# Moving the matmul operands of a decoder trunk to multiples of 256 bytes

## The chip, the cores and the metric

The kernel runs on one core of one Trainium2 chip. The metric is the device time of one execution in microseconds (us), the median over runs. The profile is one further execution, recorded by the hardware profiler.

## The reference

One decoder layer on x of 1024 positions by 1024 channels, float32. Cut to what matters:

```python
h = layer_norm(x, ln_in_g, ln_in_b)
u = h @ w_in                       # GLU halves a, g | z | x,B,C | dt | gate_a | gate_b
y_a = conformer_branch(u_glu, ...) # a*sigmoid(g), causal 31-tap depthwise conv, LN, silu, @ w_conv_out
y_b = ssd_branch(z, xbc, dt, ...)  # 4-tap conv, silu, Mamba-2 state space scan, gated RMS norm, @ w_ssm_out
mix = (sigmoid(gate_a) * y_a + sigmoid(gate_b) * y_b) @ w_o
h = layer_norm(ALPHA * h + mix, ln1_g, ln1_b)
up = causal_dwconv(h @ w_up, dw_w, dw_b)          # 1024 -> 2 * 2816 channels, 3 taps
ffn = (silu(up_gate) * up_val) @ w_down           # 2816 -> 1024
out = layer_norm(ALPHA * h + ffn, ln2_g, ln2_b)
```

## The kernel before

**Numbers as pairs.** Every large operand is kept as two halves of type `float32r`, a rounded high part and the rest (`weights` at L150, `split_to` at L181, `split_pair` at L738). A product is three matmuls (`mm3` at L164, lines 167 to 169): high by high, high by low, low by high. In `TE.matmul(ps, wa, xa)` the first operand is stationary (128 columns, loaded into the array by a LDWEIGHTS that the profile lists as PEld) and the second is moving: 512 columns streamed past it, except in `first_columns` (L349), where it is 256.

**Stages.** The positions go in two halves. For each half: `ln_in` normalises and transposes into `hT`; `mixers` runs the projections of `hT`, the 4-tap convolutions, the state space groups (`ssd_group`) and, on VectorE, the 31-tap convolution (`conv31`, L421); `combine` makes `sT` and multiplies `sT` by `w_co` and `yT` by `w_sp`. Then `out_proj` (first half) and `ffn_blocks` (second half), which also prepares the feed-forward input in blocks: `h1b1` and `h1b2` (tiles of pool `big`) and three block sums `h1s1` to `h1s3`. `up_first` and 22 calls of `up_pair` make the up projection in seven block products (a Strassen-like scheme with 4 chunks of contraction, so 12 matmuls each); their PE order is written out by hand (`tc.manual_schedule`). One of the seven uses the weights `w_s3`, which lie in pool `up`. `down` runs seven more products over 11 contraction steps each; a step takes one weight tile for both operands and 12 matmuls, and the tiles come in turn from `wsp` (left) and from pool `down` (right). `ln_out` ends the kernel.

**Order.** The framework's scheduler orders the instructions of each engine, with the priorities given in the code. Loads of weights go through SP's DMA queue.

**Where the tiles lie.** SBUF space of each partition is given out by a stack of pools from the left (the first pool begins at byte 16512) and another stack from the right (down from byte 229344). Each tile's size is rounded up to 32 bytes. A pool that is closed gives its space to the next; a tile that comes to lie on an older one waits for that one's last use. With the sizes of the code the tiles begin here, in bytes modulo 256:

| tiles | pool, side | before |
|---|---|---|
| `ident` | const, left | 128 |
| `pc` (2276 bytes, slot of 2304) | const, left | 160 |
| `hT`, `yT`, `mixT`, `h1b1`, `h1b2` | big, left | 160 |
| staged weights `st`, `ra`, `rb`, `dr` | wst, left | 160 |
| weights `w_*` | wsp, left | 160 |
| `sT` | comb, left | 160 |
| weights `w_s3` | up, left | 32 |
| block sums `h1s1` to `h1s3` | ffq, right | 224 |
| weights of every second step of `down` | down, right | 224 |
| `seg_mv`, `seg_st`, `state0` to `state3` | states, right | 224 |

All offsets within these tiles that a matmul of 512 columns uses are multiples of 512 bytes.

Lines that the prediction's steps touch: `pc` L125 and its load L251, the loads of `x` L244 and `nw` L204, the store of `x` L258, the weight loads L153, the first reader of `pc` L265.

Of the kernel before, what the change touches and what calls it, by code (L numbers as in the profile page):

```python
# [8 lines left out]
F32 = mybir.dt.float32  # L9
# [7 lines left out]
P = 128  # L17
# [24 lines left out]
PC_N = PC_FB + 44  # L42
# [14 lines left out]
def kernel(  # L57
# [15 lines left out]
    V, A, G, TE, SY = nc.vector, nc.scalar, nc.gpsimd, nc.tensor, nc.sync  # L73

    def pool(name, bufs=1, **kw):
        return tc.tile_pool(name=name, bufs=bufs, reuse_waits="tile", **kw)

    const = ctx.enter_context(tc.tile_pool(name="const", bufs=1))
# [13 lines left out]

    ident = const.tile([P, P], F32, name="ident")
    make_identity(nc, ident)
    mean_stack = ExitStack()
    mean_w = mean_stack.enter_context(pool("mean", side="right")).tile([P, P], F32, name="mean_w")
    V.memset(mean_w, 1.0 / D)
# [24 lines left out]
    V.tensor_add(kind_st, kind[:, 0:1], kind[:, 1:2])  # L122
    kind_neg = const.tile([P, 2], F32, name="kind_neg")
    V.tensor_scalar_mul(kind_neg, kind[:, 0:2], -1.0)
    pc = const.tile([P, PC_N], F32, name="pc")  # L125
    a_log = statep.tile([P, HEADS], F32, name="a_log")
    dskip = statep.tile([P, HEADS], F32, name="dskip")
    u_halo = statep.tile([P, 24, 3], F32, name="u_halo")
# [32 lines left out]
    def big_tile(name):  # L161
        return big.tile([P, 2, KD, HALF], F32R, tag="big", name=name)
# [25 lines left out]
    def transpose_to(dst, src, t, k0, n):  # L188

        for q in range(0, n, 4):  # L190
            pt = bank(0)
            for i in range(4):
                TE.transpose(
                    pt[:, i * P : (i + 1) * P], src[:, (q + i) * P : (q + i + 1) * P], ident
                )
            pv = pt.rearrange("p (k t) -> p k t", k=4)
            hi = dst[:, 0, k0 + q : k0 + q + 4, t * P : (t + 1) * P]
            lo = dst[:, 1, k0 + q : k0 + q + 4, t * P : (t + 1) * P]
            A.copy(hi, pv)
            V.tensor_tensor(out=lo, in0=pv, in1=hi.bitcast(F32), op=ALU.subtract)  # L200

    def row(pl, start, n, name, tag=None):
        r = pl.tile([P, n], F32, tag=tag or name, name=name)
        SY.dma_start(r, prow[start : start + n].partition_broadcast(P))  # L204
        return r
# [4 lines left out]
    def ln_stats(pl, tiles, name, sts=None):  # L210

        n = len(tiles)
        mv = pl.tile([P, n, 2], F32, tag="ln_mv", bufs=2, name=f"mv_{name}")
        rs = pl.tile([P, n], F32, tag="ln_rs", bufs=2, name=f"rs_{name}")
        for i, t in enumerate(tiles):
            if sts:
                st = sts[i]
            else:
                st = pl.tile([P, 2, 6], F32, tag="ln_st", bufs=2, name=f"st_{name}{i}")
                for q in range(2):  # L220
                    ln_part(pl, t, st, q)
            V.bn_aggr(out=mv[:, i, :], in_=st)  # L222
        A.activation(out=rs, in_=mv[:, :, 1], func=AF.Sqrt, bias=eps)
        V.reciprocal(out=rs, in_=rs)
        return mv, rs

    def ln_apply(t, mv, rs, i, g, b):
        V.scalar_tensor_tensor(  # L228
            out=t, in0=t, scalar=mv[:, i, 0:1], in1=g, op0=ALU.subtract, op1=ALU.mult
        )  # L230
        V.scalar_tensor_tensor(  # L231
            out=t, in0=t, scalar=rs[:, i : i + 1], in1=b, op0=ALU.mult, op1=ALU.add
        )

    def ln_in(hh):
        hT = big_tile(f"hT{hh}")
        with pool(f"lnin{hh}", side="right") as pl:
            first = hh == 0
            xts, gb = [], []
            with tc.high_priority(offset=6000):  # L240
                for t in range(4):
                    xt = pl.tile([P, D], F32, tag="x", bufs=4, name=f"x{hh}_{t}")
                    r0 = hh * HALF + t * P
                    SY.dma_start(xt, x[r0 : r0 + P, :])  # L244
                    xts.append(xt)
                    if first and t == 1:
                        gb = [row(pl, RW_ING, D, "in_g"), row(pl, RW_INB, D, "in_b")]
            if not first:
                gb = [row(pl, RW_ING, D, "in_g"), row(pl, RW_INB, D, "in_b")]
            if first:  # L250
                SY.dma_start(pc, pcol)  # L251
                SY.dma_start(a_log, prow[RW_AL : RW_AL + HEADS].partition_broadcast(P))
                SY.dma_start(dskip, prow[RW_SD : RW_SD + HEADS].partition_broadcast(P))
            for t, xt in enumerate(xts):
                with tc.high_priority(offset=(6000 - 1000 * (t // 2)) if first else 0):
                    mv, rs = ln_stats(pl, [xt], f"in{hh}_{t}")
                    ln_apply(xt, mv, rs, 0, *gb)
                    SY.dma_start(h_scr[hh][t * P : (t + 1) * P, :], xt)  # L258
                    transpose_to(hT, xt, t, 0, KD)
        return hT  # L260
# [861 lines left out]
    def ln_out(dp, t, r, g, b, st):  # L1122

        with tc.high_priority(offset=200 if t == 7 else 0):
            mv, rstd = ln_stats(dp, [r], f"f{t}", [st])
            halves = [slice(q * HALF, (q + 1) * HALF) for q in range(2)]
            for cs in halves:
                ln_apply(r[:, cs], mv, rstd, 0, g[:, cs], b[:, cs])
                SY.dma_start(out[t * P : (t + 1) * P, cs], r[:, cs])

    hT = ln_in(0)
    yT = mixers(0, hT)
    mixT = combine(0, hT, yT)
    hT = ln_in(1)
    with pool("rows0") as pl:
        rs = [pl.tile([P, D], F32, name=f"r0_{t}") for t in range(4)]
# [134 lines left out]
```

## Time and profile before

| | us |
|---|---|
| median of 3 runs (2006.31, 2008.04, 2008.36) | 2008.04 |
| the profiled execution | 2007.04 |
| its span, first to last instruction | 2005.2 |
| TensorE matmuls busy (PE, 9164) | 1971.1 |
| TensorE weight loads busy (PEld, 9164) | 1620.4 |
| VectorE busy (DVE) | 1693.9 |
| ScalarE busy (ACT) | 1022.5 |
| GpSimd busy (POOL) | 178.0 |

PEld overlaps PE. Matmuls are pipelined: the duration of one runs over into the next, so the step from one start to the next is the shorter number that fills the span. The ends of matmuls are modelled, the starts are recorded. POOL's spans are rough. The granted clock is the share of full speed that the throttle gave TensorE; its mean here is 0.998.

### The profile page before, as it was taken

How to read it: one execution, taken by the hardware profiler on the slowest of the kernel's cores; microseconds unless marked ns; L12 is line 12 of the kernel's file. 1: busy time of each engine (PE TensorE's matmuls, PEld its weight loads, DVE VectorE, ACT ScalarE, POOL GpSimd, SP SyncE). 2: the span in 40 equal slices, each digit the busy share in tenths (PEclk: the TensorE clock that was granted, in tenths of full speed). 3: DMA queues.
4: the chain of work that ended last, by engine and by line, in shares of the span. 5: the costliest groups of instructions: out<-in, count | busy, mean ns of one | idle time of the engine just before them, and what ended most of it. 6: DMA issues, size and time to landing. Idle time of an engine off the chain costs nothing. (4 is left out here: it accounts for less than half of the span.)

```text
span 2005.2 us, 24594 instructions
## 1 busy us (share of the span) xinstructions
PE 1971.1 (98%) x9164; PEld 1620.4 (81%) x9164; DVE 1693.9 (84%) x2261; ACT 1022.5 (51%) x1480; POOL 178.0 (9%) x144
## 2 busy tenths in 40 slices
PE   7999999999999999999999999999999999999998
PEld 6888888888888888888888888877778888888886
DVE  7599999979865868999998977578998878778768
ACT  4465654556453265665545546255554444553432
POOL 2010101001300000100000122001000000011000
PEclk9999999999999999999999999999999999999999
DMA  6223223233445532222323253487442232368573
GB/s 222 88 70 95 79 87 123 85 111 106 168 128 183 221 109 74 84 90 85 115 90 111 100 173 121 131 283 250 146 158 104 100 121 95 106 217 266 184 241 110
DMA packets 97031, 272.20 MB, mean 136 GB/s; under 512 B 11216, under 2 KB 11216, under 8 KB 96912
## 3 DMA queue, kind: packets, MB, share of 16 engines
q1 hardware_dynamic: 88992, 246.78, 37.2%
q0 software_dynamic: 5616, 19.66, 2.7%
q10 hardware_dynamic: 2304, 4.20, 0.6%
q8 instruction: 72, 1.18, 0.3%
q14 instruction: 47, 0.39, 0.1%
HBM read 221.05 MB, written 49.55 MB: 135 GB/s over the span
## 5 line engine op out<-in xcount | busy, mean ns | idle before, releaser
L421 DVE SCALAR_TENSOR_TENSOR c<-v,pc,c 128x512 f32<-128x512 f32 x480 | 374.5, 803 | 6.4 <-ACT c L410 5.0
L479 POOL TENSOR_TENSOR au<-seg_mv,head_of 128x1024 fp32r<-128x1024 f32 x32 | 77.0, 2408 | 958.5 <-PE sm L488 728.2
L167 PE MATMUL acc<-hT,w_c 128*128 128x512 f32 x352 | 141.1, 401 | 0.0
L168 PE MATMUL acc<-hT,w_c 128*128 128x512 f32 x352 | 140.7, 400 | 0.0
L169 PE MATMUL acc<-hT,w_c 128*128 128x512 f32 x352 | 138.5, 393 | 0.0
L910 DVE SCALAR_TENSOR_TENSOR fo<-u,pc,fo 128x1024 f32<-128x1024 f32 x88 | 111.4, 1285 | 0.4 <-ACT fo L906 0.4
L376 DVE SCALAR_TENSOR_TENSOR xbc<-u,pc,xbc 128x512 f32<-128x512 f32 x144 | 109.6, 773 | 0.7 <-ACT xbc L374 0.5
L167 PE MATMUL acc<-h1s,w_s 128*128 128x512 f32 x264 | 104.5, 396 | 2.3 <-ACT u L894 2.3
L169 PE MATMUL acc<-h1s,w_s 128*128 128x512 f32 x264 | 104.0, 394 | 0.0
L168 PE MATMUL acc<-h1s,w_s 128*128 128x512 f32 x264 | 103.5, 392 | 0.0
L167 PE MATMUL acc<-w_z,hT 128*128 128x512 f32 x256 | 100.9, 401 | 0.0
L168 PE MATMUL acc<-w_z,hT 128*128 128x512 f32 x256 | 100.9, 394 | 0.0
L169 PE MATMUL acc<-w_z,hT 128*128 128x512 f32 x256 | 100.7, 396 | 0.0
L155 ACT CAST w_c<-st_c 128x1024 fp32r<-128x1024 f32 x50 | 52.6, 1052 | 88.9 <-PE acc L169 68.1
L1049 ACT CAST w_dn<-dr 128x1024 fp32r<-128x1024 f32 (+1 forms) x73 | 60.8, 842 | 71.9 <-DVE dr L979 31.1
L1050 DVE TENSOR_TENSOR w_dn<-dr,w_dn 128x1024 fp32r<-128x1024 f32 (+1 forms) x73 | 70.1, 967 | 14.8 <-ACT w_dn L1049 14.6
L168 PEld LDWEIGHTS acc<-hT,w_c 128*128 128x128 f32 x352 | 66.1, 188 | 17.0 <-issue 3.8
L169 PEld LDWEIGHTS acc<-hT,w_c 128*128 128x128 f32 x352 | 66.1, 188 | 16.2 <-issue 2.6
L167 PEld LDWEIGHTS acc<-hT,w_c 128*128 128x128 f32 x352 | 66.1, 188 | 16.0 <-issue 2.6
L156 DVE TENSOR_TENSOR w_c<-st_c,w_c 128x1024 fp32r<-128x1024 f32 x47 | 60.5, 1288 | 20.2 <-ACT w_c L155 20.2
L167 PE MATMUL sm<-h1b,w_s 128*128 128x512 f32 x176 | 69.6, 396 | 0.0
L169 PE MATMUL sm<-h1b,w_s 128*128 128x512 f32 x176 | 69.3, 394 | 0.0
(354 smaller groups left out, 5703.1 us busy)
## 6 DMA issues: line engine op xcount, KB each, us to landing
st_c<-wcol SPq DMA_DIRECT2D x50, 512.0 KB, 3.5
st_z<-wz SPq DMA_DIRECT2D x32, 512.0 KB, 3.5
st_wo<-wo SPq DMA_DIRECT2D x24, 512.0 KB, 4.0
ra<-wup SPq DMA_DIRECT2D x22, 512.0 KB, 3.5
rb<-wup SPq DMA_DIRECT2D x22, 512.0 KB, 3.4
t_scr<-fo POOLq DMA_DIRECT2D x22, 512.0 KB, 3.4
dr<-t_scr SPq DMA_DIRECT2D x44, 256.0 KB, 4.0
dr<-wdown SPq DMA_DIRECT2D x38, 256.0 KB, 4.3
```

The costliest lines, as they stand in the source:

```text
L155: A.copy(w[:, 0, :], st)
L156: (eng or V).tensor_tensor(out=w[:, 1, :], in0=st, in1=w[:, 0, :].bitcast(F32), op=ALU.subtract)
L167: TE.matmul(ps, wa(0), xa(0), start=start, stop=False, skip_group_check=more)
L168: TE.matmul(ps, wa(0), xa(1), start=False, stop=False, skip_group_check=more)
L169: TE.matmul(ps, wa(1), xa(0), start=False, stop=stop, skip_group_check=more)
L376: V.scalar_tensor_tensor(out=o, in0=u[:, k : k + HALF], scalar=pc[:, wc + k : wc + k + 1], in1=o, op0=ALU.mult, op1=ALU.add,)
L421: V.scalar_tensor_tensor(out=accs[i], in0=v[:, k : k + HALF], scalar=pc[:, wc + k : wc + k + 1], in1=accs[i], op0=ALU.mult, op1=ALU.add,)
L479: G.tensor_tensor(out=au, in0=seg_mv[:, c, :].unsqueeze(1).to_broadcast([P, 8, P]), in1=head_of[:, g, :].unsqueeze(2).to_broadcast([P, 8, P]),
L910: V.scalar_tensor_tensor(out=o, in0=u[:, k : k + T], scalar=pc[:, wc + k : wc + k + 1], in1=o, op0=ALU.mult, op1=ALU.add,)
L1049: A.copy(w[:, 0, cs], src)
L1050: V.tensor_tensor(out=w[:, 1, cs], in0=src, in1=w[:, 0, cs].bitcast(F32), op=ALU.subtract)
```

## The change

Two pools grow by unused bytes. `pc`, the last tile of the left pool `const`, gets 24 more columns (2372 bytes, a slot of 2400 instead of 2304), and its load fills the first 569 columns as before. A new pool `edge` of 56 columns (224 bytes), which nothing reads or writes, is the first on the right side. Every tile left of the middle that is allocated after `pc` moves up by 96 bytes, every tile on the right down by 224. `ident` and the other tiles ahead of `pc` stay.

| tiles, bytes modulo 256 | before | after |
|---|---|---|
| `hT`, `yT`, `mixT`, `h1b1`, `h1b2`, `sT`, staged and split weights | 160 | 0 |
| block sums, weights of `down` on the right, states, `seg_mv`, `seg_st` | 224 | 0 |
| weights `w_s3` | 32 | 128 |

```diff
@@ -92,6 +92,8 @@
 
     ident = const.tile([P, P], F32, name="ident")
     make_identity(nc, ident)
+    edge = ctx.enter_context(pool("edge", side="right"))
+    edge.tile([P, 56], F32, name="edge")
     mean_stack = ExitStack()
     mean_w = mean_stack.enter_context(pool("mean", side="right")).tile([P, P], F32, name="mean_w")
     V.memset(mean_w, 1.0 / D)
@@ -122,7 +124,7 @@
     V.tensor_add(kind_st, kind[:, 0:1], kind[:, 1:2])
     kind_neg = const.tile([P, 2], F32, name="kind_neg")
     V.tensor_scalar_mul(kind_neg, kind[:, 0:2], -1.0)
-    pc = const.tile([P, PC_N], F32, name="pc")
+    pc = const.tile([P, PC_N + 24], F32, name="pc")
     a_log = statep.tile([P, HEADS], F32, name="a_log")
@@ -248,7 +250,7 @@
             if first:
-                SY.dma_start(pc, pcol)
+                SY.dma_start(pc[:, :PC_N], pcol)
                 SY.dma_start(a_log, prow[RW_AL : RW_AL + HEADS].partition_broadcast(P))
```

## The prediction

> **What bounds the kernel now.** I read the page first, then the waits of TensorE, then busy time by stage, then the matmuls of single tiles with their start times.
>
> ```profile
> span 2005.2 us, 24594 instructions
> PE 1971.1 (98%) x9164; PEld 1620.4 (81%) x9164; DVE 1693.9 (84%) x2261; ACT 1022.5 (51%) x1480; POOL 178.0 (9%) x144
> PEclk9999999999999999999999999999999999999999
> ```
>
> ```profile
> PE sm L193 <- DVE x L231: 14.8, 3, 12.2
> PE acc L167 <- ACT u L894: 2.3, 2, 1.2
> ```
>
> ```profile
> 100.00:510.00 410.00, 410.00 (x1965) 336.06 (x1964) 398.56 (x542) 237.84 (x374) 35.80 (x15) 1.00 0.30 96
> 700.00:1100.00 400.00, 399.82 (x1910) 328.90 (x1910) 365.17 (x511) 227.97 (x351) 32.43 (x14) 1.00 0.30 96
> 510.00:700.00 190.00, 186.68 (x898) 156.20 (x897) 135.99 (x179) 75.92 (x103) 22.30 (x14) 1.00 0.51 176
> 1100.00:1430.00 330.00, 326.00 (x1496) 266.87 (x1495) 258.41 (x333) 170.82 (x237) 38.83 (x26) 1.00 0.51 169
> 1483.00:1775.00 292.00, 292.00 (x1269) 237.94 (x1268) 237.48 (x271) 144.57 (x169) 17.28 (x28) 1.00 0.31 110
> 1775.00:1968.00 193.00, 193.00 (x843) 157.98 (x842) 148.07 (x200) 84.48 (x118) 14.44 (x26) 1.00 0.69 228
> 582.00:622.00 40.00, 40.00 (x178) 33.11 (x177) 20.52 (x26) 11.81 (x14) 0.00 (x0) 1.00 0.51 152
> 1968.00:2005.20 37.20, 27.96 (x122) 22.53 (x120) 33.68 (x66) 4.79 (x11) 0.00 (x0) 0.91 0.31 113
> ```
>
> Columns of the stages: from:to, length, then busy time and count of PE, PEld, DVE, ACT, POOL, granted clock, DMA share, GB/s. TensorE is never idle between 1483 and 1968 us at full granted clock, and the longest wait in the list is at the start. So over most of the span the time is the number of matmuls times the step from one start to the next. Exceptions: in the two mixer stages (100 to 510, 700 to 1100) VectorE is busy 97% and 91%, so a faster matmul there would soon wait for it, and the last 37 us are VectorE's layer norms. A shorter step pays in the other four stages: 898 + 1496 + 1269 + 843 = 4506 matmuls.
>
> The step is not everywhere the same. The tile views (minimum/median/maximum ns of one) and start times:
>
> ```profile
> L167 PE MATMUL acc<-sT,w_co x128: 389/389/389, 592.8 to 1299.2; 128*128 128x512 f32 x128
> L167 PE MATMUL acc<-h1s,w_s x264: 388/394/503, 1395.4 to 1782.6; 128*128 128x512 f32 x132
> L168 PE MATMUL acc<-h1s,w_s x264: 387/388/398, 1395.7 to 1782.8; 128*128 128x512 f32 x132
> L169 PE MATMUL acc<-h1s,w_s x264: 392/392/398, 1395.9 to 1783.0; 128*128 128x512 f32 x132
> ```
>
> ```profile
> 590.05 0.39 PE L167 MATMUL acc<-yT,w_sp 128*128 128x512 f32 x1
> ...
> 592.77 0.39 PE L167 MATMUL acc<-sT,w_co 128*128 128x512 f32 x1
> ...
> 1502.01 0.40 PE L167 MATMUL sm<-h1b,w_s 128*128 128x512 f32 x1
> ...
> 1504.80 0.40 PE L167 MATMUL acc<-h1s,w_s 128*128 128x512 f32 x1
> ...
> 1507.60 0.40 PE L167 MATMUL acc<-h1b,w_ue 128*128 128x512 f32 x1
> ...
> 1510.36 0.40 PE L167 MATMUL acc<-h1s,w_s 128*128 128x512 f32 x1
> ...
> 1797.94 0.39 PE L167 MATMUL acc<-w_dn 128*128 128x512 f32 x1
> ...
> 1800.70 0.39 PE L167 MATMUL acc<-w_dn 128*128 128x512 f32 x1
> ...
> 1803.43 0.39 PE L167 MATMUL acc<-w_dn 128*128 128x512 f32 x1
> ```
>
> Between the first two rows lie 12 steps, 2.72/12 = 226.7 ns each, and `sT`, `w_co` shows not one nanosecond of scatter: call that the locked step. The three products that begin at 1502.01, 1504.80 and 1507.60 have 12 matmuls each: 232.5, 233.3 and 230.0 ns. The two contraction steps of `down` from 1797.94 and 1800.70, again 12 each: 230.0 and 227.5 ns. All are 512 columns of the same type, with the same three calls of `mm3`. What differs is where the operands start. In bytes modulo 256, moving operand and stationary operand (the addresses are in the table of pools above): locked step 160 and 160; `w_s3` product 160 and 32; block sum `h1s` 224 and 160; `h1b1` with `w_ue` 160 and 160, directly behind a block sum; `down` with its own weights in the right pool 224 and 224; `down` with `wsp` weights 160 and 160. So the slow steps are those where the two operands of a matmul are 64 or 128 bytes apart modulo 256, and those just behind a change of that phase. The weights of the next matmul load while the present one streams, so I read the rows as two SBUF read streams that disturb each other less once they run in step.
>
> **The change part by part.** (1) The `edge` tile holds 224 bytes and no instruction touches it: 0. (2) `pc` grows by 96 bytes in its slot; its transfer still brings 569 columns.
>
> ```profile
> pc<-pcol SPq DMA_DIRECT2D x1, 284.5 KB, 10.8
> ```
>
> ```profile
> 35.29 0.67 ACT L265 ACTIVATE dtc<-acc,pc 32x512 f32<-32x512 f32 x1
> ```
>
> Issued within the first 6 us and landed 10.8 us later, it is there some 18 us ahead of its first reader, which covers it: 0. (3) Left and right pools come 320 bytes nearer, so two tiles of the mixers come to overlap one more tile of the input stage: `nw` with `x0_3`, and the third `v` slot with `x0_0`. That is an added wait, on SP's queue.
>
> ```profile
> 27.13 0.37 SPq L258 DMA_DIRECT2D h_scr<-x  x1
> 27.60 0.40 SPq L204 DMA_DIRECT2D nw<-prow  x1
> 36.67 0.33 SPq L153 DMA_DIRECT2D st_c<-wcol  x1
> ```
>
> ```profile
> DMA to landing us min/median/max: 2.9/6.2/8.9
> ```
>
> `nw` must now wait until the store of `x0_3`, issued at 27.13, has been read out: by the slowest landing of `x` at 36.0 us. Behind it in SP's queue is `st_c` at 36.67, held by something else. So between 0 and 0.3 us of delay, and I take 0, because 36.0 lies before 36.67. If that cover were gone, weight loads would come later and ACT's casts after them. The overlap with `x0_0` is stored long before. In the second half the same tiles overlap the other way, but the `x` loads come over 100 us after the last reader:
>
> ```profile
> L421 DVE SCALAR_TENSOR_TENSOR c<-v,pc,c x240: 709/739/2460, 100.6 to 520.5; 128x512 f32<-128x512 f32 x120
> L244 SPq DMA_DIRECT2D x<-x x8: 387/436/677, 0.8 to 640.9; - x8
> ```
>
> (4) VectorE and ScalarE read the moved tiles too. The same L421 row answers for them: its input starts at 30 different byte offsets of `v`, four bytes apart, and the median is 739 against a minimum of 709 ns. I take 0. (5) The transfers move no more bytes, and none of TensorE's two longest waits ends on one: 0.
>
> (6) The matmuls. After the change the operands in `big`, `wst`, `wsp`, `sT`, the block sums and the weights of `down` all start at 0 modulo 256. Only `w_s3` stays apart, at 128 against 0. No instruction is added or removed. Excess over the locked step, counting as the windows count: 582 to 622 is a locked stretch and counts 178 where 40/0.2267 = 176.4 start, so 1.6 of each count is edge. From 1483 to 1775 some 1267.4 matmuls at 226.7 ns make 287.3 us, so the excess is 4.7 us. From 1775 to 1968, 841.4 make 190.7 us: 2.3 us. From 1395 to 1483 the same kind of product runs; at the rate of the later stage, 4.7 x 88/292, that is 1.4 us. Together 8.4 us. What stays: in each of the 22 rounds (one for each `up_pair`) the `w_s3` product (12 x 5.8 ns = 70 ns) and the unlocked product behind it (as at 1507.60: 12 x 3.3 = 40 ns), 22 x 110 ns = 2.4 us; and a few tenths in `down` at its changes of bank. Gain 8.4 - 2.4 - 0.5 = 5.5 us. In the attention stages both operands move by the same 96 bytes and keep their distance, so I take 0 there. The bounds of that step are the rivals below, since no matmul of 512 columns starts at a multiple of 64 in this trace.
>
> The sum against the profiled execution: 2007.04 us, span 2005.2 and 1.8 around it, less 5.5, is 2001.5. It lies 1.0 below the median 2008.04 of the runs and 0.7 above the lowest, so I give 2002.
>
> **Rule against row.** The Trainium skill, "TensorE: Matmul & The Clock Gate", section "Step-by-step: what each phase is for", says that TensorE has two independent SBUF read ports and that loading the next tile's weights takes no read bandwidth from the running matmul. By that rule the distance of the two operands could cost nothing and the sum would be 2007. The rows at 1504.80 and 590.05, 233.3 against 226.7 ns, do not fit it as it stands.
>
> **The rivals.** No change: the slow steps belong to these two stages for another cause, such as what VectorE, ScalarE and the transfers do beside them, or the alternation of banks. For it: they are also the stages where the scatter is. Against it: the two `down` steps alternate in one stage under the same load and differ by 2.5 ns. Time 2007 to 2008. The page's rule above would give this outcome.
>
> Faster everywhere: the locked step itself holds a cost of a start that is not a multiple of 64. The row of the 256-column matmuls bounds it.
>
> ```profile
> L358 PE MATMUL acc<-hT,w_c x288: 277/283/386, 16.2 to 702.9; 128*128 128x256 f32 x144
> ```
>
> From 256 to 512 columns a matmul grows by 389 - 283 = 106 ns, so 512 columns alone take 212 and the step has 15 ns that do not grow with columns. If alignment took all of it, 4506 x 15 = 68 us, 1934. The nearest row, the shortest matmul of the block sums at 387 instead of 389, is 2 ns: 9 us more than my sum, 1993. I take the near end, because nothing shows an aligned start. The same page, section "Wait — 56ns, not 53.3ns?", gives 215.7 ns for back-to-back matmuls of 512 bf16 columns; by that figure the estimate would be 11 ns x 4506 = 50 us and 1957, which no run here shows.
>
> Slower: at 0 both streams start on the same 256-byte boundary in every matmul, and the attention stages, now locked at 226.7, settle at the 233.3 of the `h1s` product. Price 6.6 x 4506 = 30 us, 2032 with the gain kept. It decides from 5.5/4506 = 1.2 ns on, a step of 227.9 in `sT`, `w_co`. For it: 12 matmuls at 1504.80 hold that step evenly, so it is stable too. Against it: the distance that seems to count is unchanged there.
>
> **How the numbers follow.** Sum as worked out 0.50, its own range 1999 to 2005 (half or one and a half of the gain). No change 0.20. Faster everywhere 0.15. Slower 0.15. A measurement of this kernel tells about 0.2%, 4 us, from no change. The sum's case falls short of that in a tenth of its chance, so faster is 0.45 + 0.15, same 0.05 + 0.20, slower 0.15. The range 1988 to 2016 holds the first two, the near end of the third and the first quarter of the last, leaving out some 0.18.
>
> **What would show it.** Right: `h1s` rows with all three lines at a median of 389; `sT`, `w_co` still 389/389/389; both kinds of `down` step at 226.7 ns; the stage of the block sums about 4 us shorter; `nw` issued by 36 us and `st_c` no later than before; same instruction counts. Wrong: `sT`, `w_co` at any number other than 389, up or down, since then the start itself counts and not the distance; or `h1s` unchanged at 394/388/392.

## The result, and the profile after

Side by side on one chip, medians of seven runs each: 1999.94 us after the change (1999.11 to 2002.48) against 2007.64 us before. The ratio is 0.9969, 95% interval 0.996 to 0.9978: faster by 4.4 to 8.0 us. The profiled execution of the changed kernel took 2001.16 us, that of before 2007.04.

The page of the changed kernel, its span, busy times and granted clock:

```profile
span 1999.4 us, 24595 instructions
PE 1967.5 (98%) x9164; PEld 1624.8 (81%) x9164; DVE 1694.0 (85%) x2261; ACT 1022.5 (51%) x1480; POOL 176.3 (9%) x144
PEclk9999999999999999999999999999999999999999
```

The counts of TensorE, VectorE and ScalarE are the same, and so are the busy times of the last two to 0.1 us. TensorE alone lost 3.6 us. Its stages, in the columns of the windows view shown above:

```profile
1483.00:1775.00 292.00, 292.00 (x1282) 240.67 (x1281) 240.27 (x272) 144.29 (x168) 18.33 (x30) 1.00 0.32 114
1775.00:1968.00 193.00, 192.95 (x852) 159.53 (x851) 150.16 (x207) 87.25 (x122) 12.85 (x25) 1.00 0.67 221
```

In the same 292 us of the block sums the view counts 1282 matmuls instead of 1269, in the 193 us of `down` 852 instead of 843. TensorE's longest wait is of the old size (14.8 before):

```profile
PE sm L195 <- DVE x L233: 14.6, 3, 12.6
```

So what got shorter is the step. The tile views (lines are two higher than before: L167 is now L169), with one row of before that was not shown:

```profile
L167 PE MATMUL acc<-w_dn x160: 387/389/401, 1775.7 to 1992.4; 128*128 128x512 f32 x160
```

```profile
L169 PE MATMUL acc<-h1s,w_s x264: 387/390/505, 1395.7 to 1778.5; 128*128 128x512 f32 x132
L170 PE MATMUL acc<-h1s,w_s x264: 386/390/402, 1395.9 to 1778.8; 128*128 128x512 f32 x132
L171 PE MATMUL acc<-h1s,w_s x264: 387/390/398, 1396.2 to 1779.0; 128*128 128x512 f32 x132
L169 PE MATMUL acc<-sT,w_co x128: 388/390/390, 593.8 to 1301.8; 128*128 128x512 f32 x128
L169 PE MATMUL acc<-w_dn x160: 387/390/397, 1771.7 to 1986.3; 128*128 128x512 f32 x160
```

The first starts cut the span into parts. Up to the first block sum: 1395.4 before, 1395.7 after, 0.3 us later. From there to the first matmul of `down`: 380.3 before, 376.0 after, 4.3 us less. From the first to the last of these `down` rows: 216.7 before, 214.6 after, 2.1 us less. From there to the end 12.8 and 13.1. Together 0.3 - 4.3 - 2.1 + 0.3 = -5.8 us, the difference of the spans. In the sum, the whole gain lies in the two stages of the block sums and of `down`.

The 0.3 us ahead of them is two larger numbers that cancel. The second `dtc` starts at 706.9 instead of 704.2 us, 2.7 later, and 2.4 of these come back before the first block sum. Of the 2.7, 1.7 arise between 642 and 676 us: the granted clock from 664 to 668 us is 0.68 in this profile and 1.00 in that of before, and six matmuls there step by 426 or 427 ns. `e8_right` below has such a stretch too (0.62), while `e2_all160`, `e4_s3` and `e5_left` have none (1.00), so it follows neither the distances nor the starts. The 2.4 come back from 1327 to 1331 us, mostly because the profile of before has a wait of 1.2 us there, for the `r` of L718, that the profiles of the other kernels lack. Why it is there, no run shows.

The steps of the two stages, from the timeline:

```profile
593.10 0.39 PE L169 MATMUL acc<-yT,w_sp 128*128 128x512 f32 x1
...
595.82 0.39 PE L169 MATMUL acc<-sT,w_co 128*128 128x512 f32 x1
...
1503.55 0.40 PE L169 MATMUL acc<-h1s,w_s 128*128 128x512 f32 x1
...
1506.30 0.39 PE L169 MATMUL acc<-h1b,w_ue 128*128 128x512 f32 x1
...
1509.03 0.39 PE L169 MATMUL acc<-h1s,w_s 128*128 128x512 f32 x1
...
1511.74 0.39 PE L169 MATMUL sm<-h1b,w_s 128*128 128x512 f32 x1
```

Twelve matmuls lie between each row and the next one shown (593.10 to 595.82 too). The attention product takes 226.7 ns a step as before. The block sum at 1503.55, right behind a `w_s3` product like the one at 1504.80 before, takes 229.2 where that took 233.3; the `w_ue` product behind it 227.5 for 230.0; the block sum at 1509.03, with no `w_s3` product near, 225.8, which is the locked step within the hundredths that the starts have. In the table below a tile's step is the mean, over the tile's matmuls, from the start of each to the start of the next, without those over 245 ns (a wait); the distance is moving minus stationary operand, modulo 256 bytes.

| product | before: distance, ns | after: distance, ns |
|---|---|---|
| `sT`, `w_co` | 0, 226.67 | 0, 226.66 |
| `hT`, `w_c` | 0, 227.78 | 0, 227.50 |
| `h1s`, `w_s` | 64, 230.98 | 0, 227.89 |
| `h1b`, `w_s` (half of them `w_s3`) | 0 and 128, 231.77 | 0 and 128, 229.88 |
| `h1b`, `w_ue` | 0, 228.25 | 0, 226.80 |
| `down`, both kinds | 0, changing between 160 and 224: 229.01 | 0, no change: 226.71 |

### The profile page after: what moved, and what is told of

It is laid out like the page before. It is cut to its first block, busy times and chain, and to the rows that moved or that the text cites. A ratio compares the mean times of both kernels' runs of the same rounds, so it can differ in the third digit from the quotient of the medians.

```text
span 1999.4 us, 24595 instructions
## 1 busy us (share of the span) xinstructions
PE 1967.5 (98%) x9164; PEld 1624.8 (81%) x9164; DVE 1694.0 (85%) x2261; ACT 1022.5 (51%) x1480; POOL 176.3 (9%) x144
## 3 DMA queue, kind: packets, MB, share of 16 engines
q10 hardware_dynamic: 2304, 4.20, 0.6%
## 4 chain that ended last, share of the span: by engine, by line
PE 68%; DVE 24%; issue 4%; DMA 3%; ACT 1%; SPq 0%; POOL 0%; DVEq 0%; ACTq 0%
PE acc L169 17%; PE acc L171 17%; PE acc L170 17%; DVE c L423 8%; PE sm L170 3%; PE sm L171 3%; PE sm L169 3%; DVE xbc L378 2%; PE acc L360 1%; PE sm L537 1%; DMA st_wo<-wo 1%; PE sm L518 1%; DVE w_so L158 1%; DVE w_z L158 1%; DVE w_c L158 1%
## 5 line engine op out<-in xcount | busy, mean ns | idle before, releaser
L169 PE MATMUL acc<-hT,w_c 128*128 128x512 f32 x352 | 141.2, 401 | 0.0
L169 PE MATMUL acc<-h1s,w_s 128*128 128x512 f32 x264 | 103.5, 392 | 2.3 <-ACT u L896 2.3
L169 PE MATMUL acc<-w_z,hT 128*128 128x512 f32 x256 | 100.9, 401 | 0.0
L169 PEld LDWEIGHTS acc<-hT,w_c 128*128 128x128 f32 x352 | 66.2, 188 | 15.9 <-issue 2.6
L169 PE MATMUL sm<-h1b,w_s 128*128 128x512 f32 x176 | 69.2, 393 | 0.0
```

What stands on the lines that cost most here:

```text
L169: TE.matmul(ps, wa(0), xa(0), start=start, stop=False, skip_group_check=more)
```

## The experiments

The theory is that of the prediction: the step goes by the distance of the two operands modulo 256 bytes and by changes of their common start. The rival that remains is that a start at a multiple of 64 or 256 shortens a matmul by itself. The programs `e1_bench`, `e7_bench2` and `e9_bench3` have one run each.

### The cost by itself: e1_bench

In place of the layer, a program that gives TensorE nothing but streams of matmuls (cut):

```diff
+    for s in STATIONARY:                     # 0, 32, 160, 224 bytes
+        for name, m in zip(NAMES, STARTS):   # a..h: 0, 32, ... 224 bytes
+            for n in range(32):
+                TE.matmul(ps, sta[... from byte s ...], mv[... from byte m ...],
```

> Measures the disputed cost by itself: this kernel leaves out the whole computation and copies x to the output. Beside the copy TensorE runs 32 streams of 32 matmuls of 512 columns (f32r); within a stream the stationary operand starts at 0, 32, 160 or 224 bytes modulo 256 and the moving operand at 0, 32, ... 224. Theory (distance of the two operands modulo 256 sets the step): the step is 226.7 ns on the four streams with equal starts and up to 233 ns at some other distances, the same number for the same distance whatever the absolute starts. Rival 1 (absolute start): streams with both starts at 0 or both multiples of 64 are shorter than those at 32, 160, 224, and the distance does not order them. Rival 2 (it is the stage's other work and not the operands' addresses): all 32 streams have one step within 0.5 ns.

Stationary operand at 160 (`f`), moving operand at 96 to 224 (`d` to `h`); the timeline joins the matmuls of a stream, and the first column is the stream's start:

```profile
162.58 7.63 PE L50 MATMUL sfmd<-mv,sta 128*128 128x512 f32 x32
170.05 7.62 PE L50 MATMUL sfme<-mv,sta 128*128 128x512 f32 x32
177.51 7.44 PE L50 MATMUL sfmf<-mv,sta 128*128 128x512 f32 x32
184.79 7.63 PE L50 MATMUL sfmg<-mv,sta 128*128 128x512 f32 x32
192.26 7.50 PE L50 MATMUL sfmh<-mv,sta 128*128 128x512 f32 x32
```

From start to start by 32: 233.4 ns at 192 bytes' distance, 233.1 at 224, 227.5 at 0, and 233.4 at 32. All four stationary starts, mean of the 31 steps inside a stream:

| distance | stationary at 0 | at 32 | at 160 | at 224 |
|---|---|---|---|---|
| 0 | (clock still rising) | 227.5 | 227.4 | 227.4 |
| 32 | 233.4 | 233.4 | 233.4 | 232.9 |
| 64 | 229.2 | 229.2 | 229.2 | 228.8 |
| 96 | 233.7 | 233.7 | 233.7 | 233.7 |
| 128 | 233.5 | 233.5 | 233.5 | 233.4 |
| 160 | 234.1 | 234.1 | 234.1 | 234.1 |
| 192 | 233.3 | 233.4 | 233.4 | 233.4 |
| 224 | 233.1 | 233.1 | 233.1 | 233.2 |

The rows are constant to 0.5 ns and the columns alike: the distance orders the steps and the absolute start does not. The entry that is missing stands in `e9_bench3`: 226.67 ns with both operands at 0. Both rivals fall. Distances of both signs wrap (224 stands for +224 and -32 alike), and 128 is slow where 0 is fast, so the period is 256 bytes. Settled, the streams at 0 run at 226.67; their first few matmuls are what lifts the mean to 227.4. One row is not as firm as it looks: at 128 bytes `e7_bench2` and `e9_bench3` have 232.2 ns where this program has 233.5. They go round seven tiles instead of eight and run other streams ahead of it; which of the two counts was not tried.

### The same distance at another start: e2_all160

```diff
+    edge = ctx.enter_context(pool("edge", side="right"))
+    edge.tile([P, 16], F32, name="edge")        # pc as before
```

> The kernel before with 64 bytes of padding in the right pools, so that activations, weights, block sums and the weights of down all start at 160 modulo 256: distance 0 as in the changed kernel, but no start is a multiple of 64. Theory (distance): as the changed kernel, some 6 to 8 us under the kernel before (ratio 0.996 to 0.997), h1s rows near 389 in all three lines, both kinds of down step at 226.7 ns. Rival (the multiple of 256 itself counts): as the kernel before, ratio 1.000, h1s rows 394/388/392.

Ratio 0.9971, interval 0.996 to 0.9983; profiled span 1996.8.

```profile
L169 PE MATMUL acc<-h1s,w_s x264: 388/390/497, 1394.0 to 1776.2; 128*128 128x512 f32 x132
L169 PE MATMUL acc<-w_dn x160: 387/390/396, 1769.4 to 1983.9; 128*128 128x512 f32 x160
```

375.4 us from the first block sum to `down` and 214.5 inside it, as after the change (376.0 and 214.6). Not one of the operands named starts at a multiple of 64 bytes here. So the multiple of 256 is not what pays; 64 bytes of padding in one pool do the same.

### One half of the change: e5_left and e8_right

```diff
-    pc = const.tile([P, PC_N], F32, name="pc")
+    pc = const.tile([P, PC_N + 24], F32, name="pc")     # e5_left: this alone, with the load of 569 columns
...
+    edge.tile([P, 56], F32, name="edge")                # e8_right: this alone, with its pool
```

> One half of the change alone: only the left pools are moved (activations, weights, sT at 0), the right pools stay at 224. The block sums then stand 224 bytes from their weights, where e1_bench has 233.1 ns (64 bytes in the kernel before, 229.2), and the two kinds of down step still alternate, 0 and 224. Theory (distance and changes of phase): h1s products at 233 to 234 ns a step, 2 us slower there; down as before or worse, block-sum stage about 2 us longer: 2006 to 2011, ratio 1.000 to 1.002, nothing of the gain of the whole change. Rival (starts at a multiple of 256 shorten matmuls): a part of the gain, 2001 to 2005.

> The other half alone: only the right pools are moved (block sums and the right pool's weights of down at 0), the left pools stay at 160. The block sums then stand 96 bytes from their weights, where e1_bench has 233.7 ns, and the two kinds of down step alternate between 160 and 0. Theory: h1s products at 233 to 234 ns a step, about 2 us slower there; the change of phase in down stays, 2 us: 2006 to 2011, ratio 1.000 to 1.002. Rival (starts at a multiple of 256 shorten matmuls): a part of the gain, 2001 to 2005.

`e5_left`: ratio 1.0006 (0.9997 to 1.0015). `e8_right`: 1.0014 (1.0006 to 1.0023). First `e5_left`, then `e8_right`:

```profile
L167 PE MATMUL acc<-h1s,w_s x264: 392/396/499, 1395.5 to 1783.8; 128*128 128x512 f32 x132
L167 PE MATMUL acc<-w_dn x160: 387/391/402, 1776.8 to 1994.1; 128*128 128x512 f32 x160
```

```profile
L169 PE MATMUL acc<-h1s,w_s x264: 392/396/500, 1397.3 to 1785.5; 128*128 128x512 f32 x132
L169 PE MATMUL acc<-w_dn x160: 387/389/397, 1778.5 to 1996.9; 128*128 128x512 f32 x160
```

Neither half keeps any of the gain. The block-sum stage takes 381.3 and 381.2 us (380.3 before), `down` 217.3 and 218.4 (216.7 before). The block sums' step is 233.3 and 234.1 ns, close to the 233.1 and 233.7 that the table of distances has for 224 and 96 bytes. The stage grew by 1.0 and 0.9 where 2 were expected. By the starts the block sums did take 1.8 and 2.3 us more, and the `h1b` products gave back most of the difference: in `e5_left` those with `w_ue` (227.0 ns instead of 228.25), in `e8_right` those with `w_s` and `w_s3` (230.86 instead of 231.77), beside a wait of 0.6 us at 1401 us that is absent there.

### Apart where before was together: e3_gap

```diff
+    gap = ctx.enter_context(tc.tile_pool(name="gap", bufs=1))
+    gap.tile([P, 16], F32, name="gap")          # between big and wst
```

> The kernel before with 64 bytes between the activations and the weights: activations stay at 160, both weight pools, the block sums, sT and the weights of down go to 224. So the products of activations and weights (hT, yT, h1b) come to a distance of 64, while sT with w_co, the block sums and both kinds of down step have distance 0. Theory (distance): hT, yT and h1b products rise from 226.7 to 228 by 2 to 6 ns a step, sT with w_co stays at 226.7, block sums fall to about 227 to 228, down to 226.7. The attention stages that TensorE limits lose up to 2394 matmuls x 6 ns = 14 us, the block sums and down gain some 5: 2003 to 2020, likeliest slower by 3 to 10 us. Rival (absolute starts, none of which is a multiple of 64 here): no product of hT or yT changes by more than 0.5 ns and the time is that of the kernel before.

Ratio 1.0083, interval 1.0067 to 1.0098; profiled span 2021.5. Eleven steps of a `hT` product inside the first mixer, then three tile rows:

```profile
104.64 0.39 PE L169 MATMUL acc<-hT,w_gg 128*128 128x512 f32 x1
...
107.20 0.39 PE L171 MATMUL acc<-hT,w_gg 128*128 128x512 f32 x1
```

```profile
L169 PE MATMUL acc<-sT,w_co x128: 388/390/397, 601.3 to 1318.9; 128*128 128x512 f32 x128
L169 PE MATMUL acc<-h1s,w_s x264: 388/390/497, 1414.5 to 1800.6; 128*128 128x512 f32 x132
L169 PE MATMUL acc<-w_dn x160: 388/390/398, 1793.7 to 2008.5; 128*128 128x512 f32 x160
```

2.56/11 = 232.7 ns; over all of `hT`, `w_c` the step is 233.18 (227.78 before), of `yT`, `w_sp` 233.33, while `sT`, `w_co`, which kept its distance of 0, has 226.82. Where the weights are the moving operand and `hT` the stationary one, the distance is +64 instead of -64: `w_z`, `hT` has 229.74, as e1_bench has 229.2 at 64 and 233.4 at 192. `down` takes 214.8, as after the change. Direction and steps are those of the theory; the size is not. I expected 3 to 10 us, at most some 12, and 16.7 came (0.0083 x 2007); the median, 2022.8, lies outside the 2003 to 2020 that I gave. I had counted only the matmuls of the attention stages and taken the mixers as covered by VectorE. They are not. Second mixer, its first `dtc` and the last `hT`, `w_ga` product, before and in `e3_gap`:

```profile
L265 ACT ACTIVATE dtc<-acc,pc x2: 673/675/677, 35.3 to 704.2; 32x512 f32<-32x512 f32 x2
L167 PE MATMUL acc<-hT,w_ga x128: 387/389/792, 84.7 to 1098.3; 128*128 128x512 f32 x128
```

```profile
L267 ACT ACTIVATE dtc<-acc,pc x2: 673/676/678, 35.0 to 714.2; 32x512 f32<-32x512 f32 x2
L169 PE MATMUL acc<-hT,w_ga x128: 391/394/794, 85.0 to 1114.5; 128*128 128x512 f32 x128
```

394.1 us became 400.3, 6.2 more. The extra of the mixer's own matmuls over 226.67 ns, without steps over 245, rose from 1.5 to 8.1 us, 6.6 more, and nearly all of it arrived. The first mixer, where VectorE is busy 97%, covered no more: from its `dtc` to its last `hT`, `w_ga` product 398.7 us became 405.2.

### The last pair that is apart: e4_s3

```diff
-    us = [upp.tile([P, T + 32], F32, name=f"u{i}") for i in range(3)]
+    us = [upp.tile([P, T + n], F32, name=f"u{i}") for i, n in enumerate((8, 8, 48))]
```

> The changed kernel, with the columns of padding in the three u tiles shifted (8, 8, 48 instead of 32 each), so that w_s3 too starts at 0 modulo 256 and no pair of operands in the block-sum stage is apart. Theory (distance): the 2.4 to 2.8 us of excess that the block-sum stages still show go to under 0.5: 1997 to 1998, ratio to the kernel before about 0.995; the product of h1b with w_s3 at 226.7 ns a step, the h1s rows 389 in all three lines. Rival (what is left there is due to the alternation of banks or to the other engines' work): 1999 to 2001, the excess stays.

Ratio 0.9952 to the kernel before, interval 0.994 to 0.9965; median 1996.6, profiled span 1995.2. Tile rows and the window of the block sums:

```profile
L169 PE MATMUL acc<-h1s,w_s x264: 388/390/504, 1394.8 to 1774.5; 128*128 128x512 f32 x132
L169 PE MATMUL acc<-w_dn x160: 388/390/390, 1767.7 to 1982.3; 128*128 128x512 f32 x160
1483.00:1770.00 287.00, 287.00 (x1268) 237.82 (x1267) 238.78 (x271) 143.57 (x168) 18.08 (x28) 1.00 0.32 114
```

372.9 us from block sum to `down`, 3.1 less than after the change (0.5 of it a wait at 1401 us that is absent here); the step of `h1b`, `w_s` is 226.67 (229.88 after). With the prediction's 1.6 of edge, 1266.4 x 0.22667 = 287.1 us: the stage of 287 us holds the locked step from end to end, and nothing is left for banks or other engines. This version beats the kernel before by 9.6 us (7 to 12). Its interval and that of the change overlap; that it is also ahead of the change is read from the traces, which show where the time went.

### What is behind the distance: e7_bench2 and e9_bench3

Streams as in e1_bench, with other pairs:

```diff
+    stream("own", [(0, 0, 512), (128, 128, 512)])     # (stationary, moving, columns)
+    stream("nxt", [(128, 0, 512), (0, 128, 512)])
+    stream("chgc", [(0, 0, 512)] * 12 + [(64, 64, 512)] * 12, count=96)
+    stream("halfe", [(0, 128, 512)], half=True)       # bf16
...
```

> Measures by itself what e1_bench left open; again the whole computation is left out and x is copied to the output. Streams of 32 matmuls of 512 f32r columns. (1) Which stationary operand counts. In streams own and ownb the moving operand and its own stationary operand start at the same byte modulo 256, but the pair alternates between 0 and 128 (96 in ownb) from one matmul to the next, so that the moving operand is apart from the weights loaded beside it; nxt and nxtb are the reverse. Theory (the running stream and the load of the next weights disturb each other): own above 232 ns, nxt about 227. Rival (the matmul's own two operands count): own about 227, nxt above 232. (2) Changes of phase: chgc, chge and chgh change both operands from 0 to 64, 128 or 224 after every 12 matmuls. Theory: as in the two down steps of the kernel before, steps off 226.7 for 3 to 11 matmuls behind each change, 10 to 30 ns in all for a change; rival (only the distance counts): at most the one matmul at the change is longer. (3) Columns: the extra at 128 bytes is the same number of ns for 512, 256 and 128 columns if it belongs to a load, and shrinks with the columns if it belongs to the stream. (4) bf16 operands: an extra of a like size, or none if it belongs to four-byte elements. (5) Starts of 4 to 252 bytes: if only full agreement modulo 256 locks, 4 to 24 bytes cost too; if a row of 32 or 64 bytes is the unit, 4 to 24 cost nothing.

```profile
50.08 7.67 PE L56 MATMUL ownb<-mv,sta 128*128 128x512 f32 x32
57.59 7.53 PE L56 MATMUL nxtb<-mv,sta 128*128 128x512 f32 x32
64.95 22.14 PE L56 MATMUL chgc<-mv,sta 128*128 128x512 f32 x96
86.93 22.01 PE L56 MATMUL chge<-mv,sta 128*128 128x512 f32 x96
...
152.84 3.98 PE L56 MATMUL colya<-mv,sta 128*128 128x256 f32 x32
156.66 3.93 PE L56 MATMUL colyc<-mv,sta 128*128 128x256 f32 x32
...
174.89 7.08 PE L56 MATMUL halfa<-mvh,sth 128*128 128x512 bf16 x32
181.81 7.07 PE L56 MATMUL halfb<-mvh,sth 128*128 128x512 bf16 x32
```

The numbers are means of the steps inside a stream. (1) Neither answer came: `own` 228.8, `nxt` 230.0, `ownb` 234.0, `nxtb` 230.1 ns. A pair that changes at every matmul reaches 226.67 in neither way; `nxt` steps by 230 evenly. (2) Changes of phase cost as the theory says. `chgc` (64 bytes every 12 matmuls) takes 21.98/96 = 229.0 ns a step, the 229.01 of `down` before, whose two kinds of step were 64 bytes apart in the same rhythm: 24 x 2.3 = 55 ns for the two changes. Even the single steps agree: `down` at 1797.94 us before, and `chgc` behind a change, both step by 229, 229, 233, 236, 224, 231, 236, 228, 233, 231 (in `chgc` 230) and then 227 or 226 ns. `chgh` (224 bytes) has 229.2. A change by 128 (`chge`) costs less, 11 ns: two steps of 233 and 231, then 226.7 again. (3) The extra at 128 bytes is gone with 256 columns: 120.0 at distance 0 (settled), 117.9 at 64, 118.4 at 128; with 128 columns all three settle at 111.7. (4) bf16 has none: 215.8 to 216.2 at 0, 32, 64, 128 and 192 bytes. (5) Starts 4, 8, 16 and 24 bytes apart cost too (235, 233, 232 and 233 ns; the first without its opening step of 423 ns, right behind the bf16 streams), and so do 48 to 252 bytes (229.6 to 233.3): of all the distances tried, only 0 modulo 256 locks.

The Trainium skill, "TensorE: Matmul & The Clock Gate", section "Wait — 56ns, not 53.3ns?", has 215.7 ns for 512 columns; the bf16 streams agree (215.8). The four-byte type of this kernel does not reach it, even locked. The same page, section "Step-by-step: what each phase is for", has the load of weights take no SBUF read bandwidth from the running matmul: the bf16 streams, the same at all five distances, agree. For the four-byte type the step depends on where the two operands lie (233 against 226.7 ns at equal work); whether the load takes bandwidth there, no run here shows.

```diff
+    stream("scy...", [(0, m)], m_cols=64)                  # 64 stationary columns
+    stream("wown", [(x, x) for x in walk])                 # walk: 0, 32, ... 224
+    stream("wnext", [((x - 32) % 256, x) for x in walk])
...
```

> Measures by itself whether the load of weights is the second party; the whole computation is left out and x is copied to the output. Streams of 64 matmuls of 512 f32r columns. (1) The stationary operand has 128, 64 or 32 columns, so that a load of weights is whole, half or a quarter, at distances of 0, 32, 64, 128 and 192 bytes modulo 256. Theory (the load disturbs the running stream): the extra at 32, 128 and 192, 6.6 ns at 128 columns, shrinks about with the load, to 3 to 4 ns at 64 columns and 1 to 2 at 32. Rival (the distance of the two starts counts and the size of the load does not): 6 to 7 ns at all three. (2) salt changes only the stationary operand, from 0 to 128 and back at each matmul, malt only the moving one: if the steps go by distance alone, both have the mean of 226.7 and 233.4, 230 ns. (3) Both operands walk by 32 bytes a matmul; in wown the moving operand stands at the start of its own weights, in wnext at that of the next weights, in wprev at that of the weights before. Theory (next weights): wnext is the lowest of the three, by over 2 ns; rival (own weights): wown is; if a steady start is needed, all three are near 230 or above.

```profile
34.60 14.67 PE L46 MATMUL scxa<-mv,sta 128*128 128x512 f32 x64
49.11 15.10 PE L46 MATMUL scxb<-mv,sta 128*128 128x512 f32 x64
...
108.51 14.89 PE L46 MATMUL scya<-mv,sta 128*64 128x512 f32 x64
123.23 14.95 PE L46 MATMUL scyb<-mv,sta 128*64 128x512 f32 x64
```

On (1) both theories miss. With half the load the step at distance 0 does not stay at 226.7 while the extra shrinks; it rises, from 226.7 (34.60 to 49.11, 64 steps) to 230.0 with 64 columns (108.51 to 123.23) and 231.6 with 32, and at 32 bytes it is 231.1 and 233.0. So the number of stationary columns matters, which may speak for the load as part of the pattern (it also sets how many rows of output are written), but fewer columns break the lock instead of easing it. (2) `salt` has 233.3, `malt` 229.9 (230 expected of both). (3) `wown` 234.2, `wnext` and `wprev` 230.9: the walk picks out neither the next weights nor the own ones, and all three stay near 230 or above, as was expected if a steady start is needed. Which two accesses meet is left open. What stands is narrower: with this type, 512 columns and 128 stationary columns, a stream of matmuls falls into a step of 226.67 ns if both operands start at the same byte modulo 256 and go on starting there. Otherwise its single steps lie between 224 and 241 ns, with means from 227.5 (a common change by 128 every 12 matmuls) to 235 ns.

## Why the prediction was right

Its forecast was 2002.0; the sum from profiled execution to profiled execution was 2001.5, and the changed kernel's took 2001.16. It was worked out as a gain of 5.5 us, and the spans differ by 5.8. That these agree within 0.3 us is partly luck: the medians of the two kernels differ by 7.7, the seven runs of each by some 3.5 us among themselves, and the 5.8 hold the 2.7 and the -2.4 us of above, which the sum does not have and which cancel. The stages are the firmer test. By its points:

**Edge, `pc`, transfers, VectorE and ScalarE at 0.** Busy times of VectorE and ScalarE moved by 0.1 and 0.0 us. `dtc`, first reader of `pc`, starts at 35.7 instead of 35.3 us. All before the first block sum together came out 0.3 us later, which is the 2.7 and the -2.4 of above and no proof that each of these terms is 0.

**The added wait of `nw`.** It came, and was covered as forecast. SP's queue after:

```profile
27.59 0.44 SPq L260 DMA_DIRECT2D h_scr<-x  x1
34.30 0.33 SPq L206 DMA_DIRECT2D nw<-prow  x1
37.11 0.33 SPq L155 DMA_DIRECT2D st_c<-wcol  x1
```

`nw` went out 6.70 us later, below the bound of 36.0. `st_c` is 0.44 later than before, but the store ahead of `nw` is 0.46 later already (27.59 for 27.13) and does not wait for it. The delay has another source, and `nw` adds nothing that shows.

**The matmuls.** By the prediction's own count the excess of 1483 to 1775 is now 292 - 1280.4 x 0.22667 = 1.8 us (4.7 before), that of 1775 to 1968 192.95 - 850.4 x 0.22667 = 0.2 (2.3 before). By first starts, the block sums gave back 4.3 where 3.7 were worked out (6.1 less the 2.4 that stay), and `down` 2.1 where 1.8 were: both terms were sized somewhat low.

**What stays.** 2.4 us were put on the `w_s3` pair and the product behind it. `e4_s3` removed that pair and saved 3.1 us of the stage. Of this 0.5 is a wait at 1401 us that its profile lacks, so 2.6 stand against the 2.4.

**Attention at 0.** `sT`, `w_co` keeps 226.66 ns.

Three things in it did not hold. It named as its own mark of failure that `sT`, `w_co` show any number but 389; the rows show 388/390/390. The recorded starts say that the step did not move (226.66 ns), and `e2_all160`, where `sT` starts at 160 as before, shows the same 390, so it is not the new start. The mark was wrong: a modelled duration can shift by 1 ns without the step. Why it did is open. For the same reason the `h1s` rows have a median of 390 and not the 389 that it named. Its reading of the cause, two read streams that disturb each other, is no more than it was: the number of stationary columns has a part in it, but not the one that reading predicts. And 233.3 ns, which it took as a stable step of the block sums, is not what their distance settles at: at 64 bytes the long streams run at 229.2, and the block sums of before have a mean of 230.98. The 12 matmuls at 1504.80 did step evenly, but they stand right behind a `w_s3` product and are too few to show what it settles at.

Of the rivals, no change falls with the ratio, and faster everywhere with `e1_bench`, where streams at multiples of 64 are not shorter than others. Slower falls with the rows of `sT`; its size, a step of 233 in the attention stages, is what `e3_gap` brings about by a distance of -64 bytes, at 16.7 us. The 30 us put on it took all 4506 matmuls as products of 512 columns and left the mixers out.

## What to carry to other kernels

With four-byte operands, group the matmuls of a trace by the bytes at which their two operands start, modulo 256, before looking for other causes of a few ns in the step; then place the pools so that both operands agree and neighbouring products have the same start. Here 64 bytes of padding in one place did as much as 320 in two, padding only one of the two sides gave nothing or a loss, and 64 bytes in the wrong place cost 0.8%. And a second engine that is busy 97% of a stage does not hide a loss of the one that is busy 100%: in `e3_gap` each mixer grew by over 6 us. Before a stage is counted as covered, ask what a longer step would do there as well as a shorter one.

## What the runs showed of the hardware

- The step of a matmul of 512 four-byte columns with 128 stationary columns: 226.67 ns at distance 0, 229.2 at 64 bytes, 232 to 234 at the other multiples of 32, whatever the absolute start. +64 and -64 differ (229.2 and 233.4).
- Behind a change of both starts from 0 to 64 bytes it takes ten matmuls to lock again, behind the change back three, behind a change by 128 two.
- With 256 columns the step at distance 0 is the longer one (120.0 against 117.9 at 64 bytes); with bf16 all five distances lie between 215.8 and 216.2 ns.
- With fewer stationary columns the step at distance 0 gets longer, 226.7, 230.0 and 231.6 ns for 128, 64 and 32.
